# Band attention on one core: where the key projection and the modulation steps run between the scores

## Chip, cores and metric

The kernel runs on one core of one Trainium2 chip. Time is device time in microseconds (us); a run's time is that of the one core. Lower is better.

## The reference

A trunk of two layers on 512 tokens of width 1024: a gated linear recurrence with a feed-forward block, then chunked band attention with a feed-forward block. Every sub-layer has an RMS norm whose scale and shift come from a conditioning vector `c`. The part that matters here is the attention, 16 heads of width 64:

```python
k, v = jnp.split(u_kv @ w_kv, 2, axis=-1)          # one shared K/V
q = u @ w_q
s = jnp.einsum('bqhd,bkhd->bhqk', qc, kb) * scale + bias   # chunk of 64, own + 8 past chunks
s = jnp.where(valid, s, MASK_VALUE)
p = jax.nn.softmax(s, axis=-1)
o = jnp.einsum('bhqk,bkhd->bqhd', p, vb)
mix = o @ w_o
h = h + g1 * mix                                   # g1, sc2, sh2, ... = c_act @ mod_w + mod_b
u = modulate(rms_norm(h, norm_ffn), sh2, sc2)      # input of the feed-forward block
```

All inputs are float32 and the kernel keeps that precision: each matrix product is made of three products of reduced-precision parts.

## The kernel before

Activations lie transposed, channels on the 128 partitions, in 8 tiles `h[j]` of 128x512. A weight block is 8 tiles of 128x128. It is loaded as one 128x1024 row block (`raw`, 512 KB, asked for on SyncE's DMA queue), and `split` makes two parts of it: the high part `wh` on ScalarE (ACT, L147) and the low part `wl = raw - wh` on VectorE (DVE, L153). `mm3` (L239 to L241) then issues three matmuls for each of the 8 tiles: high x high, high x low of the activation, low x high. A projection of 512 tokens is thus 8 steps of 3 matmuls of 512 columns. Each of `raw`, `wh` and `wl` has three buffers, so the part of one weight block waits for the block three before it.

The program is traced in the order in which the Python code runs. A planner then orders each engine's instructions by that order, but moves a later one ahead where, by the planner's own times, the earlier one is not ready yet. `tc.issue_after(ins)` holds the instructions traced under it, where they run on the engine of `ins`, behind `ins`. On the chip each engine runs its list in that order.

**Attention** (L1509 to L1686) is one loop over 64 units: 16 heads times 4 blocks of 128 queries, so 8 units for a pair of heads. In unit k the loop traces

- `scores(hd, i)`: two matmuls of the query part with the high and the low key part (L1572, L1573), then on DVE the bias and row maximum (L1576), on ACT the exponential (L1579), on DVE the reciprocal and the scaling of the rows (L1580, L1581);
- `transposes` of the unit three before (L1590) and their copy to SBUF (L1595 on ACT, L1597 on DVE);
- five units behind the last of a pair, `output(p)`: 16 matmuls with the values (L1604);
- at some units (`MODS_AT`) one step of `side`, described below;
- projection steps from the generator `bfiller`: values, then for each pair p the key projection `("k", p)`, the key copies, the query projection `("bq", p)`, the query copies, and behind pair 7 the first six steps of output blocks 0 to 2 (`("bo", n)`). `CREDIT` and `RATES` say how many steps a unit takes: 3.5 up to unit 16, then 2.0 up to unit 56, then 1.5. A step of three matmuls belongs to one `yield`. `hold` keeps the copies of a pair back until its buffers can be free.

The query copies (L1553 to L1556) make, for head a, `ta` = [high part; low part] and the same for head b in `tb`: ACT writes the high part of `ta`, ACT the high part of `tb`, then DVE the low part of `ta` (L1555) and the low part of `tb` (L1556). All four read the one PSUM tile `pq`. The first score of a pair needs `ta` whole.

Behind the loop comes the **output projection**: for each of 8 output blocks n the rest of its matmuls (blocks 0 to 2 have two steps left, block 3 onwards all eight, with the weights split in `proj`), then on DVE the residual (L405), on ACT the square (L283, for n = 0 L279), on DVE the sum of squares (L286), and the split of the scaled input of the feed-forward block (`us3h` on ACT, L320; its low part on DVE, L321). Then `early_pair` starts the feed-forward block (tiles named `e_f`).

**Modulation steps.** `mod_vectors(("sc2b", "sh2b"))` is a generator, `side`, of 16 steps after a first call that only asks for a row. A step asks for the next 512 KB row of the modulation matrix on SyncE's queue (L378, two buffers) and multiplies the present one on DVE with a sum over the row (L389, tile `mw`), held behind the DVE instruction in `state["mods_after"]`. Before, `MODS_AT` makes 13 calls within the loop (four in each of pairs 0 and 1, one in each of pairs 2 to 6), so 12 steps, and the remaining four are taken in the output projection, behind the residuals of blocks 0 to 3.

Of the kernel before, what the change touches and what calls it, by code (L numbers as in the profile page):

```python
# [12 lines left out]
AF = mybir.ActivationFunctionType  # L13
# [46 lines left out]
HELD, FREE, MOVED = (6, 7), 12, (3, 4)  # L60


V1_AFTER, CREDIT, RATES = 1, 3.0, (3.5, 16, 2.0, 56, 1.5)


KEEP = 5
# [9 lines left out]
def trunk(ctx: ExitStack, tc: tile.TileContext, d, out):  # L76
# [49 lines left out]
    def by_transfer(key):  # L126

        if key[0] == f"f{OUT}" and key[1] == "o":
            return key[2] in MOVED
        return key[0] in [f"f{layer}" for layer in FAST] and key[1] == PLAIN - 1  # L130

    def split(raw, nk, n, nm, tag, key):
        if key in spare:
            wh, wl = spare.pop(key)()
        elif key[:2] == (f"f{OUT}", "o") and key[2] in HELD:
            wh, wl = (wp.tile([P, SHIFT + D], F32R, tag=tag + x, name=f"{nm}_{x}")[:, NEAR:NEAR + nk * n]
                      .rearrange("p (k c) -> p k c", k=nk) for x in "hl")
        else:
            wh = wp.tile([P, nk, n], F32R, tag=tag + "h", name=f"{nm}_h")
            wl = wp.tile([P, nk, n], F32R, tag=tag + "l", name=f"{nm}_l")  # L140
        if by_transfer(key):
            A.activation(wl, raw, AF.Copy, scale=-1.0)
            state["moved"] = G.dma_start(out=wl, in_=raw, accum_op=ALU.add)
        with ExitStack() as pinned:
            if "unit" in state and key[0] in ("k", "bq"):
                pinned.enter_context(tc.issue_after(state["mods_after"].ins))
            A.activation(wh, raw, AF.Copy)  # L147

            state.pop("meanwhile", lambda: None)()
            if key == ("ao", 0):  # L150
                pinned.enter_context(tc.issue_after(state["advanced"].ins))
            if not by_transfer(key):
                low = V.tensor_sub(wl, raw, wh)  # L153
        if not by_transfer(key):
            if key[0] in ("av", "g", "zf", "q", "ao") or key[1] == "o":
                state["mods_after"] = low
        return wh, wl
# [75 lines left out]
    def mm3(ps, w, kt, u, start, stop):  # L233
        wh, wl = w
        uh, ul = u
        with ExitStack() as pinned:
            if "behind" in state:
                pinned.enter_context(tc.issue_after(state["behind"].ins))
            T.matmul(ps, wh[:, kt, :], uh, start=start, stop=False)  # L239
        T.matmul(ps, wh[:, kt, :], ul, start=False, stop=False)  # L240
        T.matmul(ps, wl[:, kt, :], uh, start=False, stop=stop)  # L241

    def proj(key, u, res, ahead=SPLIT_AHEAD):
        w = weight(key, ahead)
        ps = bank("_".join(str(x) for x in key))
        for kt in range(KT):
            mm3(ps, w, kt, u[kt], kt == 0, kt == KT - 1)
            if kt == KT - 1:
                res.append(ps)
            yield  # L250
# [144 lines left out]
    def drain(gen):  # L395
        for _ in gen:
            pass
# [4 lines left out]
        return a  # L402

    def residual(j, ps, g, c=slice(0, S)):
        state["residual"] = V.scalar_tensor_tensor(h[j][:, c], ps[:, c], g[:, j:j + 1], h[j][:, c], op0=ALU.mult,  # L405
                                                   op1=ALU.add)

    def fast_inputs(fp, rb, a, sh, nm):

# [1099 lines left out]
    with tc.tile_pool(name="attn", bufs=1) as ap:  # L1509
# [17 lines left out]
        def qk(p):  # L1527
# [22 lines left out]
            yield p  # L1550
            ta = ap.tile([P, S], F32R, tag="ta", name=f"ta{p}", bufs=2)
            tb = ap.tile([P, S], F32R, tag="tb", name=f"tb{p}", bufs=2)
            A.activation(ta[Q1], pq[Q1], AF.Copy, scale=sc)  # L1553
            A.activation(tb[Q2], pq[Q2], AF.Copy, scale=sc)
            V.scalar_tensor_tensor(ta[Q2], pq[Q1], sc, ta[Q1], op0=ALU.mult, op1=ALU.subtract)  # L1555
            V.scalar_tensor_tensor(tb[Q1], pq[Q2], sc, tb[Q2], op0=ALU.mult, op1=ALU.subtract)  # L1556
            heads[2 * p] = (ta, ka, kla)
            heads[2 * p + 1] = (tb, kb, klb)
# [7 lines left out]
        def scores(hd, i):  # L1566
# [2 lines left out]
            nm = f"{hd}_{i}"  # L1569
            ps = bank("s" + nm)  # L1570
            c = slice(i * P, (i + 1) * P)
            T.matmul(ps[:, 0:n], tq[:, c], kk[:, 0:n], start=True, stop=False)  # L1572
            T.matmul(ps[:, 0:n], tq[:, c], kl[:, 0:n], start=False, stop=True)  # L1573
            s = sm.tile([P, S], F32, tag=("sq", "ut")[i % 2], name="sb" + nm, bufs=2)
            st = ap.tile([P, 4], F32, tag="st", name="st" + nm, bufs=4)
# [76 lines left out]
        part = []  # L1652
        fill = bfiller()
        side = mod_vectors(("sc2b", "sh2b"))
        LAG, LAG2 = 3, 4
        MODS_AT = ((0, 2, 4, 6),) * 2 + ((2,),) * 5 + ((),) * 2
        units = [(hd, i) for hd in range(BH) for i in range(NB)]
        live = {}
        credit = CREDIT
# [5 lines left out]
        for k in range(len(units) + LAG2 + 1):  # L1665
# [17 lines left out]
            while credit >= 1 and (hold is None or k >= 8 * (hold - 1) - 1):  # L1683
                hold = next(fill, None)
                credit -= 1
        drain(fill)  # L1686
        acc = sm.tile([P, S], F32, tag="nacc", name="acc3", bufs=1)
        a_f1 = gain_scale(C_NF + KT, mod["sc2b"], "a_f1")
        shifts[("f1", 0, 0)] = shifts[("f1", 0, 1)] = mod["sh2b"]
        us = []  # L1690
        for n in range(KT):
# [8 lines left out]
            residual(n, ps, mod["g1b"])  # L1700
            square_into(acc, n, "n3")
            us.append(scaled(n, a_f1[:, n:n + 1], "us3"))
            if n < 4:
                state["mods_after"] = state["residual"]
                next(side, None)
            if n == 3:
                drain(side)

                with tc.issue_after(state["scaled"].ins):
                    A.activation(csig[:, 0:1], cols[:, 0:1], AF.Silu)  # L1710
# [236 lines left out]
```

## Time and profile before

| | before |
|---|---|
| median of 3 runs | 1224.31 us (1223.09 to 1225.62) |
| profiled execution, its own time | 1226.39 us |
| its span, first to last instruction | 1224.3 us |
| granted TensorE clock, mean | 0.995 |
| PE / DVE / ACT busy | 1202.3 / 1011.0 / 671.3 us |
| attention loop from the first score to the last output | 677 to 840 us |
| output projection to the first `e_f` matmul | 840 to 881 us |

The profile is one execution of the program. Engines: PE is TensorE's matmuls, PEld its weight loads, DVE VectorE, ACT ScalarE, POOL GpSimd, SPq SyncE's DMA queue. A line number such as L1555 is that of the kernel before. In a timeline row stand the start, the duration, engine, line, operation, output and inputs, shape, and in brackets the idle time of that engine just before and what ended it. Matmuls are pipelined: a 512-column matmul is shown with 0.39 us, and the next one starts earlier than that.

### The profile page before, as it was taken

The page shows a single profiled execution, that of the slowest core. Times are in us where ns is not written, and L with a number is a line of the kernel's source. Part 1 is how long each engine was busy: PE and PEld are TensorE (multiplying, and loading weights), DVE is VectorE, ACT ScalarE, POOL GpSimd, SP SyncE. Part 2 cuts the span into 40 slices and gives each one's busy share as a digit, 9 for nine tenths or more (in the row PEclk, how much of TensorE's full clock was granted, in tenths as well). Part 3 has the DMA queues.
Part 4 walks back from the last instruction along what each step waited for, and adds up shares of the span by engine and source line. Part 5 has one row for each costly group of instructions (what it writes and reads, how often), then busy time and mean ns, then how long its engine had stood idle before and what let it go on. Part 6 is the DMA issues. An engine that isn't in the chain of part 4 may idle for free.

```text
span 1224.3 us, 22314 instructions
## 1 busy us (share of the span) xinstructions
PE 1202.3 (98%) x8758; PEld 1054.2 (86%) x8758; DVE 1011.0 (83%) x1821; ACT 671.3 (55%) x1204; POOL 51.1 (4%) x59
## 2 busy tenths in 40 slices
PE   8999999999999999999999999997999999999997
PEld 6887788888899999988888877775789999998997
DVE  8997778788989999986689778896787888887984
ACT  6455446444656566742238566674455656666553
POOL 0100000000000000000001101010000000001100
PEclk9999999999999999999999999998999999999999
DMA  9642354364423433468766977682634556446842
GB/s 354 251 131 99 114 180 156 108 214 162 131 96 136 138 127 139 143 222 271 239 217 175 276 215 196 195 211 89 194 97 156 189 199 203 168 137 153 228 121 95
DMA packets 71402, 211.94 MB, mean 173 GB/s; under 512 B 7553, under 2 KB 10241, under 8 KB 71297
## 3 DMA queue, kind: packets, MB, share of 16 engines
q1 hardware_dynamic: 63952, 194.27, 46.7%
q0 software_dynamic: 7200, 15.99, 7.9%
q8 instruction: 68, 1.11, 0.4%
q14 instruction: 38, 0.30, 0.1%
q10 hardware_dynamic: 144, 0.26, 0.1%
HBM read 204.99 MB, written 20.97 MB: 185 GB/s over the span
## 4 chain that ended last, share of the span: by engine, by line
PE 82%; DVE 9%; ACT 4%; issue 2%; DMA 2%; SPq 0%; POOLq 0%; ACTq 0%; DVEq 0%
PE f_r L642 9%; PE f_r L641 9%; PE f_r L640 9%; PE f_o L240 4%; PE f_o L241 4%; PE f_o L239 4%; PE f_or L832 2%; PE f_or L831 2%; PE f_or L830 2%; PE o L1162 1%; PE g L239 1%; PE g L241 1%; PE av L262 1%; PE f L241 1%; PE ao L239 1%
## 5 line engine op out<-in xcount | busy, mean ns | idle before, releaser
L642 PE MATMUL f_r<-f_h,f_w_l 128*128 128x256 f32 x1008 | 278.7, 276 | 0.0
L641 PE MATMUL f_r<-f_l,f_w_h 128*128 128x256 f32 x1008 | 278.7, 276 | 0.0
L640 PE MATMUL f_r<-f_h,f_w_h 128*128 128x256 f32 x1008 | 278.7, 276 | 0.0
L641 PEld LDWEIGHTS f_r<-f_l,f_w_h 128*128 128x128 f32 x1008 | 189.5, 188 | 0.1
L640 PEld LDWEIGHTS f_r<-f_h,f_w_h 128*128 128x128 f32 x1008 | 189.3, 188 | 0.1
L642 PEld LDWEIGHTS f_r<-f_h,f_w_l 128*128 128x128 f32 x1008 | 189.3, 188 | 0.0
L389 DVE SCALAR_TENSOR_TENSOR mw<-mw,crow 128x1024 f32<-128x1024 f32 x96 | 115.6, 1219 | 0.4 <-DMA mw<-in_modw 0.4
L590 ACT ACTIVATE f_w_h<-f_x 128x1024 fp32r<-128x1024 f32 x72 | 76.8, 1066 | 50.6 <-PE f_r L641 39.1
L591 DVE TENSOR_TENSOR f_w_l<-f_x,f_w_h 128x1024 fp32r<-128x1024 f32 x72 | 88.2, 1226 | 8.6 <-ACT f_w_h L590 5.2
L591 DVE TENSOR_TENSOR f_w_l<-r_f_c,f_w_h 128x1024 fp32r<-128x1024 f32 x72 | 68.8, 955 | 22.9 <-ACT f_w_h L590 22.9
L590 ACT ACTIVATE f_w_h<-r_f_c 128x1024 fp32r<-128x1024 f32 x72 | 61.1, 849 | 46.6 <-PE f_r L641 46.6
L147 ACT ACTIVATE f_o_h<-r_f_o 128x1024 fp32r<-128x1024 f32 (+2 forms) x39 | 34.3, 891 | 70.5 <-PE f_o L240 48.5
L240 PE MATMUL f_o<-f_p,f_o_h 128*128 128x512 f32 x176 | 68.6, 390 | 0.0
L241 PE MATMUL f_o<-f_p,f_o_l 128*128 128x512 f32 x176 | 68.5, 390 | 0.0
L239 PE MATMUL f_o<-f_p,f_o_h 128*128 128x512 f32 x176 | 68.3, 389 | 0.0
L1579 ACT ACTIVATE sb<-sb,st 128x128 f32<-128x128 f32 (+1 forms) x64 | 35.8, 560 | 37.3 <-DVE st L1578 36.6
L153 DVE TENSOR_TENSOR f_o_l<-r_f_o,f_o_h 128x1024 fp32r<-128x1024 f32 (+2 forms) x35 | 36.1, 1035 | 22.4 <-ACT f_o_h L147 22.1
L1065 DVE TENSOR_TENSOR kq<-kq,t 128x1024 f32<-128x1024 f32 x28 | 34.2, 1222 | 8.1 <-PE l L1132 3.3
L241 PEld LDWEIGHTS f_o<-f_p,f_o_l 128*128 128x128 f32 x176 | 33.0, 188 | 7.4 <-DVE f_o_l L153 0.5
L240 PEld LDWEIGHTS f_o<-f_p,f_o_h 128*128 128x128 f32 x176 | 33.0, 188 | 7.0 <-DVE f_p L542 0.3
L239 PEld LDWEIGHTS f_o<-f_p,f_o_h 128*128 128x128 f32 x176 | 33.0, 188 | 6.8
L241 PE MATMUL f<-f_h,f_l 128*128 128x512 f32 x96 | 36.9, 391 | 0.1
(517 smaller groups left out, 3220.5 us busy)
## 6 DMA issues: line engine op xcount, KB each, us to landing
mw<-in_modw SPq DMA_DIRECT2D x96, 512.0 KB, 4.4
r_f_c<-in_ffn_in SPq DMA_DIRECT2D x72, 512.0 KB, 3.4
ws<-in_ffn_in SPq DMA_DIRECT2D x18, 512.0 KB, 6.4
ws<-in_ffn_in POOLq DMA_DIRECT2D x18, 512.0 KB, 8.3
f_x<-ws SPq DMA_DIRECT2D x36, 256.0 KB, 2.8
mrow<-in_modw SPq DMA_DIRECT2D x16, 512.0 KB, 8.2
r_f<-in_ffn_in SPq DMA_DIRECT2D x16, 512.0 KB, 4.1
r_f_o<-in_ffn_out SPq DMA_DIRECT2D x16, 512.0 KB, 3.5
```

The source lines that it names most:

```text
L147: A.activation(wh, raw, AF.Copy)
L153: low = V.tensor_sub(wl, raw, wh)
L239: T.matmul(ps, wh[:, kt, :], uh, start=start, stop=False)
L240: T.matmul(ps, wh[:, kt, :], ul, start=False, stop=False)
L241: T.matmul(ps, wl[:, kt, :], uh, start=False, stop=stop)
L389: V.scalar_tensor_tensor(mw, mw, 1.0, crow, op0=ALU.mult, op1=ALU.mult, accum_out=raw[:, j:j + 1])
L590: A.activation(wh, raw, AF.Copy)
L591: V.tensor_sub(wl, raw, wh)
L640: T.matmul(ps, wh[:, j, :], uh, start=f, stop=False, skip_group_check=True)
L641: T.matmul(ps, wh[:, j, :], ul, start=False, stop=False, skip_group_check=True)
L642: T.matmul(ps, wl[:, j, :], uh, start=False, stop=stop and j == 3, skip_group_check=True)
L1579: A.activation(s[:, 0:n], s[:, 0:n], AF.Exp, bias=st[:, 1:2], accum_out=st[:, 2:3])
```

## The change

Four edits.

1. In the attention loop, at the last unit of pairs 1 to 5, the generator is drawn until step 4 of the next but one key projection has been traced (`FIRST = 4`, so 5 steps, 15 matmuls), and the first score matmul of pairs 2 to 6 is held behind the last of these. The rate for units 16 to 55 goes from 2.0 to 1.375 steps a unit, so the remaining 3 key steps and 8 query steps of a pair are spread over its 8 units.
2. The query copies are traced in the order: high part of `ta`, low part of `ta`, high part of `tb`, low part of `tb`.
3. The high part of the weights of output block 2 is held behind the high part of `ta` (of pair 7), its low part behind the low part of `ta`.
4. `MODS_AT` has one more step in each of pairs 2 to 5, which makes 17 calls: all 16 steps lie in the loop, and `drain(side)` stands ahead of the output projection; the four steps behind the residuals of blocks 0 to 3 are gone.

```diff
-V1_AFTER, CREDIT, RATES = 1, 3.0, (3.5, 16, 2.0, 56, 1.5)
+V1_AFTER, CREDIT, RATES = 1, 3.0, (3.5, 16, 1.375, 56, 1.5)
@@ split
+            if key == ("bo", 2):
+                pinned.enter_context(tc.issue_after(state["queries"][0].ins))
             A.activation(wh, raw, AF.Copy)
...
+            if key == ("bo", 2):
+                pinned.enter_context(tc.issue_after(state["queries"][1].ins))
             if not by_transfer(key):
                 low = V.tensor_sub(wl, raw, wh)
@@ mm3
-        T.matmul(ps, wl[:, kt, :], uh, start=False, stop=stop)
+        return T.matmul(ps, wl[:, kt, :], uh, start=False, stop=stop)
@@ proj
-            mm3(ps, w, kt, u[kt], kt == 0, kt == KT - 1)
+            state["fill"] = key, kt, mm3(ps, w, kt, u[kt], kt == 0, kt == KT - 1)
@@ qk
-            A.activation(ta[Q1], pq[Q1], AF.Copy, scale=sc)
+            state["queries"] = (
+                A.activation(ta[Q1], pq[Q1], AF.Copy, scale=sc),
+                V.scalar_tensor_tensor(ta[Q2], pq[Q1], sc, ta[Q1], op0=ALU.mult, op1=ALU.subtract))
             A.activation(tb[Q2], pq[Q2], AF.Copy, scale=sc)
-            V.scalar_tensor_tensor(ta[Q2], pq[Q1], sc, ta[Q1], op0=ALU.mult, op1=ALU.subtract)
             V.scalar_tensor_tensor(tb[Q1], pq[Q2], sc, tb[Q2], op0=ALU.mult, op1=ALU.subtract)
@@ scores
-            T.matmul(ps[:, 0:n], tq[:, c], kk[:, 0:n], start=True, stop=False)
+            with ExitStack() as pinned:
+                if state["fill"][0] == ("k", hd // 2 + 1) and not hd % 2 and not i:
+                    pinned.enter_context(tc.issue_after(state["fill"][2].ins))
+                T.matmul(ps[:, 0:n], tq[:, c], kk[:, 0:n], start=True, stop=False)
@@ the loop over units
-        LAG, LAG2 = 3, 4
-        MODS_AT = ((0, 2, 4, 6),) * 2 + ((2,),) * 5 + ((),) * 2
+        LAG, LAG2, FIRST = 3, 4, 4
+        MODS_AT = ((0, 2, 4, 6),) * 2 + ((2, 4),) * 4 + ((2,),) + ((),) * 2
...
+            if at == 7 and 0 < p < KT - 2:
+                while state["fill"][:2] != (("k", p + 2), FIRST):
+                    hold = next(fill, None)
         drain(fill)
+        drain(side)
@@ output projection
-            if n < 4:
-                state["mods_after"] = state["residual"]
-                next(side, None)
             if n == 3:
-                drain(side)
```

`residual` no longer keeps its instruction in `state["residual"]`, which nothing else used.

More of the change, by code (lines that the diff above doesn't have):

```diff
@@ L404, in residual @@
     def residual(j, ps, g, c=slice(0, S)):
-        state["residual"] = V.scalar_tensor_tensor(h[j][:, c], ps[:, c], g[:, j:j + 1], h[j][:, c], op0=ALU.mult,
-                                                   op1=ALU.add)
+        V.scalar_tensor_tensor(h[j][:, c], ps[:, c], g[:, j:j + 1], h[j][:, c], op0=ALU.mult, op1=ALU.add)
     def fast_inputs(fp, rb, a, sh, nm):
```

## Prediction

> **What bounds the kernel now.** I read the head of the page first: which engine is busy, and who ends the chain of waits.
>
> ```profile
> span 1224.3 us, 22314 instructions
> PE 1202.3 (98%) x8758; PEld 1054.2 (86%) x8758; DVE 1011.0 (83%) x1821; ACT 671.3 (55%) x1204; POOL 51.1 (4%) x59
> PE 82%; DVE 9%; ACT 4%; issue 2%; DMA 2%; SPq 0%; POOLq 0%; ACTq 0%; DVEq 0%
> ```
>
> TensorE (PE) sets the time; only 22 us of the span are not PE's by the page, and 9% of the chain is VectorE (DVE). The change touches no arithmetic, so it can gain only what PE waits or runs slow inside attention and the output projection behind it. The view by stretches, cut at the first score of a head pair and around the start of the output projection, says where that is:
>
> ```profile
> core 0: us, PE busy (x) PEld busy (x) DVE busy (x) ACT busy (x) POOL busy (x), PEclk, DMA share, GB/s
> 762.25:781.25 19.00, 18.59 (x101) 14.38 (x101) 15.52 (x53) 12.93 (x30) 1.54 (x2) 1.00 0.77 193
> 800.25:820.30 20.05, 19.18 (x102) 14.67 (x103) 19.14 (x58) 15.90 (x36) 3.16 (x3) 1.00 0.85 225
> 842.87:857.62 14.75, 8.52 (x27) 6.17 (x26) 12.10 (x17) 6.24 (x9) 0.00 (x0) 0.77 0.57 195
> ```
>
> A pair of heads (first row: pair 4) costs 19.0 us and PE idles a little in it. In pair 6 (second row) DVE is at 95%. In the third stretch PE is busy 8.5 of 14.75 us and its granted clock falls to 0.77: that is the big hole. PE's timeline gives both places exactly (columns: start, duration, and in brackets the idle time before it and who ended it):
>
> ```profile
> 725.87 0.33 PE L1572 MATMUL s<-ka,ta 128*128 128x128 f32 x1 [0.25 <-DVE ta L1555]
> 762.25 0.33 PE L1572 MATMUL s<-ka,ta 128*128 128x128 f32 x1 [0.43 <-DVE ta L1555]
> 781.25 0.33 PE L1572 MATMUL s<-ka,ta 128*128 128x128 f32 x1 [0.41 <-DVE ta L1555]
> 800.25 0.33 PE L1572 MATMUL s<-ka,ta 128*128 128x128 f32 x1 [0.41 <-DVE ta L1555]
> 820.30 0.33 PE L1572 MATMUL s<-ka,ta 128*128 128x128 f32 x1 [0.87 <-DVE ta L1555]
> ```
>
> ```profile
> 844.72 0.39 PE L239 MATMUL bo<-oh,bo_h 128*128 128x512 f32 x1
> 845.40 0.39 PE L240 MATMUL bo<-ol,bo_h 128*128 128x512 f32 x1
> 847.92 0.50 PE L239 MATMUL bo<-oh,bo_h 128*128 128x512 f32 x1 [2.12 <-ACT bo_h L147]
> 848.26 0.39 PE L240 MATMUL bo<-ol,bo_h 128*128 128x512 f32 x1
> 852.75 0.80 PE L241 MATMUL bo<-oh,bo_l 128*128 128x512 f32 x1 [4.11 <-DVE bo_l L153]
> 857.62 0.41 PE L240 MATMUL bo<-ol,bo_h 128*128 128x512 f32 x1
> 872.17 0.39 PE L239 MATMUL bo<-oh,bo_h 128*128 128x512 f32 x1
> 881.01 0.39 PE L239 MATMUL e_f<-us3h,f_h 128*128 128x512 f32 x1
> ```
>
> From 872.17 to 881.01 lie 39 matmuls of 512 columns: 0.227 us each, start to start. A shown duration of 0.39 overlaps the next, so 0.16 us is added to each bracket to get PE time lost. First scores of pairs 2, 4, 5, 6, 7 lose 0.41, 0.59, 0.57, 0.57, 1.03: 3.17 us together, all on the scaled query's low part (ta, L1555). In the second fence, 844.72 is the first matmul of output block n = 3 and 881.01 is the first behind block 7: 5 blocks of 24 = 120 matmuls, 27.2 us at 0.227. They take 36.29, so **9.1 us** are lost: two waits (2.29 and 4.26, start to start) and 11 steps of 0.44 instead of 0.227 behind them (2.4). PE works on the high halves of three blocks and then stands until the low half of block 3's weights (bo_l, L153) exists.
>
> **Part 1: all 16 modulation steps inside attention; none in the output projection.** Why bo_l was late is in the timelines of DVE and ScalarE (ACT):
>
> ```profile
> 842.64 2.01 ACT L147 ACTIVATE bo_h<-r_bo 128x1024 fp32r<-128x1024 f32 x2 [1.46 <-PE bo L240]
> 845.08 0.71 ACT L320 ACTIVATE us3h<-h,a_f 128x512 fp32r<-128x512 f32 x1
> 842.87 0.75 DVE L405 SCALAR_TENSOR_TENSOR h<-bo,mod_g1b,h 128x512 f32<-128x512 f32 x1 [0.96 <-PE bo L241]
> 843.54 1.21 DVE L389 SCALAR_TENSOR_TENSOR mw<-mw,crow 128x1024 f32<-128x1024 f32 x1
> 845.35 1.21 DVE L389 SCALAR_TENSOR_TENSOR mw<-mw,crow 128x1024 f32<-128x1024 f32 x1
> 849.08 1.21 DVE L389 SCALAR_TENSOR_TENSOR mw<-mw,crow 128x1024 f32<-128x1024 f32 x1
> 851.48 3.49 DVE L153 TENSOR_TENSOR bo_l<-r_bo,bo_h 128x1024 fp32r<-128x1024 f32 x3
> ```
>
> bo_h of block 3 is finished at about 843.7 (half of the first row), but its low half runs on DVE only at 851.48, behind three modulation products (mw) of 1.21 us and the residuals, squares and splits of blocks 0 to 2. In program order all of these stand ahead of bo_l; the planner takes the earliest ready one, and with the products in the row DVE never ran dry. Without them: residual 0 ends at 843.54; residual 1 can run about 843.6 to 844.3 (PE closes block 1 six matmuls before 844.72); the next item in order, the split of block 0, needs us3h, not ready before 845.79. So DVE is empty at 844.3 and takes bo_l of block 3: 844.3 to 845.5. PE needs it at 844.72 + 2 x 0.227 = 845.18, and two high-half matmuls of block 4 can fill in. bo_l of block 4 has until 850.6; DVE's six other items of 0.75 at most fit before it with nothing to spare. I leave 0.6 us of waits for both: gain 9.1 - 0.6 = **8.5 us**. Ends: 9.1 (nothing left), and 1.6 if DVE keeps its order without filling the gap (second rival). I take a value near the upper end, as DVE's own rows leave it empty there. The fourth product (behind block 3) hid beside PE; nothing for it.
>
> The clock decides 2.4 of the 9.1. A shorter gap further on bears on this:
>
> ```profile
> 886.40 1.05 PE L291 MATMUL n_ss<-mean,acc 128*128 128x1 f32 x8 [1.15 <-DVE acc L286]
> 888.70 0.63 PE L241 MATMUL e_f<-us3h,f_l 128*128 128x512 f32 x1
> 891.26 0.63 PE L241 MATMUL e_f<-us3h,f_l 128*128 128x512 f32 x1
> ```
>
> Between 888.70 and 891.26 six steps take 0.427 each: a slow stretch after a gap of 1.3 us and eight one-column matmuls. So a left-over wait could still bring slow steps; at 0.6 us I expect none, and 2.4 more lost is the lower end (gain 6.1). The Trainium skill, "TensorE: Matmul & The Clock Gate", section on HAM oscillation, says that only PE-idle gaps over about 3.4 us bring the half clock back. By that rule a wait of 0.6 us costs only itself (8.5 stands); by the row at 886.40 it could cost up to 2.4 more; the gap of 4.3 us at 852.75 agrees with the rule, the one at 886.40 is shorter than it allows.
>
> The four products move into pairs 2 to 5, one more each: 1.21 us and a result read of 0.08 on DVE, 15.52 + 1.3 = 16.8 of about 18.4 us per pair (91%). Their weight rows (4 x 512 KB) are asked for earlier on SyncE's queue, with a row buffer that the pair before has freed. On PE's path this costs nothing as long as DVE stays ahead; pair 6 ran at 95% and lost PE time only at its end. I charge 0.1 us in each of five pairs, 0.5 in all, between 0 and the 0.57 that a pair loses today. Nearest is 0: in the stretch that gets tighter I put the first query-weight matmul that needs a low half at about 4.9 us behind the pair's first score (three units with their transposes 1.8, three key steps 2.2, the fourth score 0.5, two matmuls 0.5). Its low half in pair 5:
>
> ```profile
> 784.77 1.22 DVE L153 TENSOR_TENSOR bq_l<-r_bq,bq_h 128x1024 fp32r<-128x1024 f32 x1
> ```
>
> It ends at 785.99, 4.74 behind the score at 781.25. That was needed 8 us behind before; now it is just in time. Whatever is late there costs tenths.
>
> **Part 2: 15 key matmuls ahead of a pair's first score (pairs 2 to 6), the rest one step to a unit.** PE's work is the same, only its order changes. Today the planner put 11 matmuls ahead of pairs 4 to 6 and 15 or 16 ahead of pairs 2 and 3. Four more are 0.91 us, over the 0.57 to 0.59 lost in pairs 4 to 6: covered. Pair 2 has its 16 already; there part 3 must do it.
>
> **Part 3: the query's low part between the two copies.**
>
> ```profile
> 798.29 0.58 ACT L1553 ACTIVATE ta<-bq 64x512 fp32r<-64x512 f32 x1
> 798.88 0.59 ACT L1554 ACTIVATE tb<-bq 64x512 fp32r<-64x512 f32 x1
> 799.51 0.68 DVE L1555 SCALAR_TENSOR_TENSOR ta<-bq,ta 64x512 fp32r<-64x512 f32 x1 [0.40 <-ACT tb L1554]
> 816.52 1.05 ACT L147 ACTIVATE bo_h<-r_bo 128x1024 fp32r<-128x1024 f32 x1
> 818.23 1.22 DVE L153 TENSOR_TENSOR bo_l<-r_bo,bo_h 128x1024 fp32r<-128x1024 f32 x1
> 819.56 0.69 DVE L1555 SCALAR_TENSOR_TENSOR ta<-bq,ta 64x512 fp32r<-64x512 f32 x1
> ```
>
> ta's low part does not need tb, yet the third row waits for it (both read one PSUM tile). With the low part issued between them it can start 0.3 to 0.6 us sooner; head b's query is ready no later. So pair 2's 0.41 is covered as well. Pair 7 has no key matmuls. There bo_l of block 2 (fifth row) sits ahead of ta; pinned behind it, it frees 1.2 us: ta's low part would run 818.8 to 819.5, against 819.56 to 820.25. With bo_h out of the way on ACT somewhat sooner still. Of the 1.03 I take 0.85. bo_l of block 2 then runs later in pair 7, where its matmuls come behind two others; no cost.
>
> Sum for parts 2 and 3: 0.41 + 0.59 + 0.57 + 0.57 + 0.85 = 3.0. All together 8.5 + 3.0 - 0.5 = **11.0 us**. The sum is made in the execution with the span of 1224.3 us, which took 1226.39 with what lies around it; the median of three runs is 1224.31. Taken off that median: **1213.3**.
>
> **Rivals.**
> 1. *DVE keeps the old order at the tail* (residuals, squares and splits of blocks 0 to 2, then bo_l). Only the products drop out, and the splits still wait for ACT: bo_l would start between 847.9 (851.48 - 3 x 1.21) and 849.9. PE gains 1.6 to 3.6 there, and perhaps 1.5 of slow steps. With 2.5 from the pairs: about 1218. For it: the planner's times are not the chip's. Against it: DVE has nothing else at 844.3.
> 2. *DVE becomes the bound in pairs 2 to 5.* If its idle time stays at 19.00 - 15.52 = 3.5 us, a pair takes 16.8 + 3.5 = 20.3 us, 1.3 longer than now: 4 x 1.3 = 5.2 lost instead of 2 gained; with the tail's 8.5 and pair 7's 0.85, about 1220. For it: DVE and ACT take their items in the planned order and wait for each other (0.40 ahead of 799.51). Against it: the 5.5 us of projections between a pair's last score and the next pair's first now let DVE run clear.
> 3. *Slower: the row loads hold up weight loads.* SyncE's queue is in order, and a row load stands until DVE has used the row two before it:
>
> ```profile
> SPq L378 <- DVE mw L389: 58.2, 12, 24.9
> ```
>
> 12 such waits, up to 24.9 us. If in pairs 2 to 5 a key or query weight is asked for behind one and lands late, PE waits openly. It decides from 11 / 4 = 2.75 us a pair; with 5 us a pair it is 1224.3 - 11.0 + 20 = 1233. Against it: today's long wait falls in a stretch with nothing else to ask for, and high halves are made nearly a pair early.
> 4. *Part 2 does nothing* because ACT's copies are late by as much as the score: 1.7 us less gain, 1215.0, inside the first case's range.
>
> **How the numbers follow.** The forecast case (both holes closed, 1210 to 1216.5, with the fourth rival in it) 0.64; rival 1 (1216.5 to 1219.5) 0.18; rival 2 (1219 to 1223) 0.09; rival 3 0.04; better than 1210 0.05, since DVE may also be less late ahead of the gap at 886.40 (1.3 us and 1.3 of slow steps). The range 1209.0 to 1219.5 holds the first two and most of the last. 0.2% is 2.4 us, about what a measurement of this kernel tells from none (three runs spread over 2.5). Faster by more: 0.64 + 0.18 + 0.05 + 0.03 of rival 2 = 0.90; within: 0.06; slower: 0.04.
>
> **What would show it.** The profile after should have no bracket over 0.2 us at the first scores of pairs 2 to 7; no product (L389) between the last attention output and block 3; bo_l of block 3 on DVE within 2 us of its bo_h; granted clock 1.00 through the output projection, and about 27.5 us from block 3's first matmul to the first behind block 7. Wrong would be: DVE still full from residual 0 to bo_l of block 3, pairs 3 to 5 of 19 us or more, or PE waiting for bq_l or k_l inside a pair.

## The result and the profile after

The change takes 0.73% off: median 1214.97 us (1213.83 to 1216.16, six runs) against 1223.84 us for the kernel before (1222.39 to 1225.62, six runs). The ratio is 0.9927, 95% interval 0.9915 to 0.994. The forecast was 1213.3 us, with a range of 1209.0 to 1219.5. The time is near the forecast, but the profile shows that the output projection gave somewhat more than forecast and attention, forecast 2.5 us shorter, became 0.9 us longer, so the parts are read one by one. Line numbers of the kernel after are 2 to 7 higher than before: L239 to L241 are L243 to L245, L389 is L393, L1555 is L1558.

The head of the page after, with the shares of the chain of waits:

```profile
span 1213.6 us, 22300 instructions
PE 1199.2 (99%) x8758; PEld 1052.1 (87%) x8758; DVE 1008.5 (83%) x1821; ACT 670.4 (55%) x1204; POOL 51.0 (4%) x59
PE 85%; DVE 7%; ACT 2%; issue 2%; DMA 2%; SPq 0%; POOL 0%; POOLq 0%; ACTq 0%; DVEq 0%
```

PE is idle in 14 us of the span, where before it was in 22. The view by stretches, cut as before, at the first scores of pairs 4, 5, 6 and 7, and from block 3 of the output projection to the first `e_f`:

```profile
core 0: us, PE busy (x) PEld busy (x) DVE busy (x) ACT busy (x) POOL busy (x), PEclk, DMA share, GB/s
763.44:782.37 18.93, 18.45 (x102) 14.41 (x101) 16.06 (x54) 12.47 (x30) 1.25 (x2) 1.00 0.82 202
782.37:801.30 18.93, 18.45 (x101) 14.42 (x101) 16.06 (x54) 12.47 (x30) 2.17 (x2) 1.00 0.71 208
801.30:820.04 18.74, 17.13 (x93) 12.62 (x92) 17.26 (x57) 15.31 (x36) 1.06 (x1) 1.00 0.76 227
846.06:873.26 27.20, 27.20 (x122) 22.41 (x121) 23.43 (x41) 15.05 (x22) 2.09 (x2) 1.00 0.68 196
```

The last row is the output projection: 27.20 us and PE busy in all of them at full clock, where before took 36.29. The big hole is closed to the last tenth. DVE and ACT at its place:

```profile
844.22 1.43 DVE L409 SCALAR_TENSOR_TENSOR h<-bo,mod_g1b,h 128x512 f32<-128x512 f32 x2 [0.94 <-PE bo L245]
845.57 1.22 DVE L157 TENSOR_TENSOR bo_l<-r_bo,bo_h 128x1024 fp32r<-128x1024 f32 x1
846.70 0.75 DVE L409 SCALAR_TENSOR_TENSOR h<-bo,mod_g1b,h 128x512 f32<-128x512 f32 x1
843.99 2.01 ACT L149 ACTIVATE bo_h<-r_bo 128x1024 fp32r<-128x1024 f32 x2 [1.44 <-PE bo L244]
```

Two residuals, then `bo_l` of block 3, then the third residual: the order that the prediction worked out.

The first three rows of the stretches are the surprise. A pair still takes 18.93 us, with half a microsecond of PE idle in it. PE's waits moved from the pair's first score to its query projection:

```profile
730.97 0.51 PE L245 MATMUL bq<-uqh,bq_l 128*128 128x512 f32 x1 [0.22 <-DVE st L1585]
750.11 0.50 PE L245 MATMUL bq<-uqh,bq_l 128*128 128x512 f32 x1 [0.28 <-DVE bq_l L157]
769.05 0.50 PE L245 MATMUL bq<-uqh,bq_l 128*128 128x512 f32 x1 [0.48 <-DVE bq_l L157]
787.98 0.50 PE L245 MATMUL bq<-uqh,bq_l 128*128 128x512 f32 x1 [0.48 <-DVE bq_l L157]
806.91 0.50 PE L245 MATMUL bq<-uqh,bq_l 128*128 128x512 f32 x1 [0.48 <-DVE bq_l L157]
818.18 0.50 PE L244 MATMUL bo<-ol,bo_h 128*128 128x512 f32 x1 [0.94 <-DVE ol L1629]
820.04 0.33 PE L1579 MATMUL s<-ka,ta 128*128 128x128 f32 x1 [0.19 <-DVE ta L1558]
```

The waits at the first scores are gone except for pair 7 (last row). In their place PE waits in each of pairs 2 to 6 at its first matmul with the low half of the query weights, and once at the end of pair 6 for the low part of an attention output. With 0.16 us for each bracket, as in the prediction, that is 4.2 us, more than the 3.17 us that were there before. Of it 2.7 us stand at `bq_l` and 1.45 us ahead of pair 7.

### The profile page after: what moved, and what is told of

Its sections match the earlier page's. It is cut to its first block, busy times and chain, and to the rows that moved or that the text cites. A ratio compares the mean times of both kernels' runs of the same rounds, so it can differ in the third digit from the quotient of the medians.

```text
span 1213.6 us, 22300 instructions
## 1 busy us (share of the span) xinstructions
PE 1199.2 (99%) x8758; PEld 1052.1 (87%) x8758; DVE 1008.5 (83%) x1821; ACT 670.4 (55%) x1204; POOL 51.0 (4%) x59
## 3 DMA queue, kind: packets, MB, share of 16 engines
q8 instruction: 68, 1.11, 0.4%
## 4 chain that ended last, share of the span: by engine, by line
PE 85%; DVE 7%; ACT 2%; issue 2%; DMA 2%; SPq 0%; POOL 0%; POOLq 0%; ACTq 0%; DVEq 0%
PE f_r L644 9%; PE f_r L645 9%; PE f_r L643 9%; PE f_o L244 4%; PE f_o L243 4%; PE f_o L245 4%; PE f_or L835 2%; PE f_or L834 2%; PE f_or L833 2%; PE bo L1611 1%; PE av L266 1%; PE f L245 1%; PE f L243 1%; PE bo L243 1%; PE f L244 1%
## 5 line engine op out<-in xcount | busy, mean ns | idle before, releaser
L393 DVE SCALAR_TENSOR_TENSOR mw<-mw,crow 128x1024 f32<-128x1024 f32 x96 | 115.7, 1219 | 2.0 <-DMA mw<-in_modw 2.0
L245 PE MATMUL f_o<-f_p,f_o_l 128*128 128x512 f32 x176 | 68.5, 390 | 0.0
L243 PE MATMUL f_o<-f_p,f_o_h 128*128 128x512 f32 x176 | 68.3, 389 | 0.0
L245 PEld LDWEIGHTS f_o<-f_p,f_o_l 128*128 128x128 f32 x176 | 33.0, 188 | 7.4 <-DVE f_o_l L157 0.5
L243 PEld LDWEIGHTS f_o<-f_p,f_o_h 128*128 128x128 f32 x176 | 33.0, 188 | 6.8
L245 PE MATMUL f<-f_h,f_l 128*128 128x512 f32 x96 | 36.9, 391 | 0.3 <-DMA f_l<-r_f 0.3
```

Source lines behind the costliest of these rows:

```text
L245: return T.matmul(ps, wl[:, kt, :], uh, start=False, stop=stop)
L393: V.scalar_tensor_tensor(mw, mw, 1.0, crow, op0=ALU.mult, op1=ALU.mult, accum_out=raw[:, j:j + 1])
```

## The experiments

For each run two lengths of the profile are given: **attention**, from the first score of pair 0 to the start of the last group of value matmuls, and the **tail**, from there to the first `e_f` matmul. Each ratio is to runs of the kernel before that were made together with the run's own.

| run | median us | ratio to before, 95% | attention | tail |
|---|---|---|---|---|
| before (lengths of its first profile) | 1223.84 | 1 | 161.08 | 42.85 |
| after | 1214.97 | 0.9927 (0.9915 to 0.994) | 162.01 | 33.73 |
| e1 steps only | 1213.08 | 0.992 (0.9907 to 0.9932) | 160.39 | 33.72 |
| e2 order only | 1221.03 | 0.9982 (0.9973 to 0.9991) | 159.04 | 42.97 |
| e3 old queries | 1214.97 | 0.9935 (0.9923 to 0.9948) | 162.33 | 33.72 |
| e4 steps late | 1212.43 | 0.9913 (0.9899 to 0.9926) | 160.55 | 33.77 |
| e5 before again | 1222.83 | one run | 161.01 | 42.79 |
| e6 steps behind block 3 | 1211.73 | 0.9911 (0.9896 to 0.9926) | 159.38 | 33.77 |
| e7 one step left | 1219.24 | 0.9973 (0.9961 to 0.9984) | 159.35 | 39.68 |
| e8 steps later | 1212.64 | 0.9917 (0.9902 to 0.9932) | 159.01 | 34.46 |
| e9 late, old queries | 1213.55 | 0.9918 (0.9904 to 0.9931) | 160.54 | 33.76 |
| e10 second at 3 | 1215.43 | 0.9935 (0.9922 to 0.9947) | 162.08 | 33.78 |
| e11 second at 6 | 1213.35 | 0.9918 (0.9904 to 0.9931) | 160.21 | 33.74 |
| e12 second at 0 | 1218.24 | 0.9957 (0.9944 to 0.9969) | 164.78 | 33.72 |

An interval reaches some 1.5 us to either side, so differences below about 2 us between two of these medians are not told apart; the lengths are read from one execution each and are finer.

**e1: part 1 alone.** The kernel before, with the new `MODS_AT`, `drain(side)` ahead of the output projection, and no steps in it.

```diff
-        MODS_AT = ((0, 2, 4, 6),) * 2 + ((2,),) * 5 + ((),) * 2
+        MODS_AT = ((0, 2, 4, 6),) * 2 + ((2, 4),) * 4 + ((2,),) + ((),) * 2
+        drain(side)
-            if n < 4:
-                state["mods_after"] = state["residual"]
-                next(side, None)
             if n == 3:
-                drain(side)
```

> The kernel before with the 16 modulation steps inside attention (MODS_AT and drain as after), nothing else. Theory A (the products alone closed the hole in the output projection): block 3 to the first e_f matmul takes 27.2 to 28 us instead of 36.3, the gap ahead of the row sums goes as well, and the whole is 1211 to 1214, as fast as the full change or a little faster, because the rest gained nothing. Rival B (the new score order carries part of it): 1216 or more, with 1 to 3 us still lost in the projection or at the first scores.

Measured: 0.992, so part 1 alone is at least as fast as the whole change. The tail is 33.72 us, the same as after. And with the old order of matmuls the four extra products cost nothing in attention: 160.39 us, 0.7 less than before. In this order the first matmul with `bq_l` comes 7.7 to 8.4 us behind a pair's first score, and `bq_l` ends at 4.53, so there is room. Three first scores still wait (0.42, 0.61 and 0.31 us with the 0.16, pairs 2, 3 and 7).

**e2: parts 2 and 3 alone.** The kernel after, with twelve steps in the loop and four behind residuals 0 to 3, as before.

```diff
-        MODS_AT = ((0, 2, 4, 6),) * 2 + ((2, 4),) * 4 + ((2,),) + ((),) * 2
+        MODS_AT = ((0, 2, 4, 6),) * 2 + ((2,),) * 5 + ((),) * 2
-        drain(side)
+            if n < 4:
+                state["mods_after"] = state["residual"]
+                next(side, None)
             if n == 3:
+                drain(side)
```

(In e2, e6 and e7 `residual` keeps its instruction in `state["residual"]` again.)

> The changed kernel with the modulation steps as before (12 in the loop, four in the output projection). Theory A (the low half of the next query weights comes just too late for PE because the score order and the query order moved its need forward and its making back): still 0.3 to 0.7 us of PE wait for bq_l in pairs 3 to 6, attention no shorter than before, the hole in the projection as before, whole 1222 to 1226. Rival C (the four extra products on VectorE are what delays it): waits for bq_l under 0.2 us, attention 2 to 3 us shorter than before, whole 1219 to 1222.

Measured: attention 159.04 us, 2.04 less than before. A pair without the extra product:

```profile
780.89:799.36 18.47, 18.47 (x102) 14.37 (x100) 15.10 (x52) 12.54 (x29) 1.04 (x1) 1.00 0.64 183
```

PE is busy in the whole of it; the forecast implied 19.00 - 0.57 = 18.43. So the new order does what it was costed for, and adding the four products to it costs 162.01 - 159.04 = 2.97 us. The waits that come with them are 2.36 us at `bq_l` in pairs 3 to 6 and 0.81 us more ahead of pair 7 (pair 2's 0.38 us is there in e2 too), 3.17 us together. Neither part is at fault alone; they collide.

**e3: part 3 undone**, the query copies back in their old order, the rest as after.

```diff
-            state["queries"] = (
-                A.activation(ta[Q1], pq[Q1], AF.Copy, scale=sc),
-                V.scalar_tensor_tensor(ta[Q2], pq[Q1], sc, ta[Q1], op0=ALU.mult, op1=ALU.subtract))
+            high = A.activation(ta[Q1], pq[Q1], AF.Copy, scale=sc)
             A.activation(tb[Q2], pq[Q2], AF.Copy, scale=sc)
+            state["queries"] = (high, V.scalar_tensor_tensor(ta[Q2], pq[Q1], sc, ta[Q1], op0=ALU.mult,
+                                                             op1=ALU.subtract))
```

> The changed kernel with the query copies in the old order (both high parts on ScalarE, then both low parts on VectorE). Theory A: VectorE no longer idles 0.66 us between the two low parts, the first softmax of a pair and bq_l come 0.3 to 0.5 us earlier behind the first score, PE's wait for bq_l falls from 0.64 to 0.2 or less, but the first score may wait up to 0.3 us again for ta; whole 0 to 2 us faster than the changed kernel (1213 to 1215). Rival D (the query order is what covers the first scores, as forecast): first scores wait 0.3 us or more in each of pairs 2 to 7 and the whole is 1 to 3 us slower than the changed kernel.

Measured: 1214.97 us, attention 0.32 us longer than after: not told apart in time. Pair 2's first score waits 0.42 us again (with the 0.16), as it does in e1 and e9 and in no kernel with the new order of copies. So part 3 removes that wait. The waits at `bq_l` fall to 0.22 to 0.37 us a pair, though, and the one ahead of pair 7 for the attention output rises to 1.40; what part 3 is worth is e9's question.

**e4: the four extra steps late**, in and behind pair 7.

```diff
-        MODS_AT = ((0, 2, 4, 6),) * 2 + ((2, 4),) * 4 + ((2,),) + ((),) * 2
+        MODS_AT = ((0, 2, 4, 6),) * 2 + ((2,),) * 5 + ((0, 4),) + ((0, 2),)
```

> The changed kernel with the four extra steps not in pairs 2 to 5 but two in pair 7 and two behind it, where VectorE has 5 us and more of idle time. Rival C (the extra products delay bq_l): waits for bq_l gone, 1211 to 1213. Theory A (order, not load): waits for bq_l within 0.2 us of those of the changed kernel, whole within 1 us of it, unless the products reach into the output projection again and bring back part of its hole.

Measured: 0.9913; pairs 3 to 5 take 18.46 to 18.51 us without a wait, as in e2, and the tail stays at 33.77. Taking the second product out of pairs 2 to 5 brings their time back. Pair 2 has a wait of its own here (1.27 us at the same matmul), and PE waits 0.70 us ahead of pair 7 for the low part of an attention output.

**e5: the kernel before, profiled again.** No edit.

> The kernel before, unchanged, profiled a second time. In the profile of before the stretch from the first fast-layer matmul (e_f) to n_b is 15.75 us, in the four kernels with the change or a part of it 12.78 to 12.87, and DVE waited 4.41 us there for a row load (r_f). Theory A: that load was late in this one execution and the change has no part in it: the stretch is again 12.8 us, the span 1221 to 1222 and attention 161 us, with the hole of 9.1 us unchanged. Rival: the hole in the output projection makes that load late: 15 to 16 us again, and a part of the change's gain lies there.

The load was late in the first execution only. DVE's wait for it, in the first profile of before, in the second, and after:

```profile
873.43 0.29 DVE L213 TENSOR_SCALAR wsh_f<-r_f,mod_sh2b 128x128 f32<-128x128 f32 x1 [4.41 <-DMA r_f<-in_ffn_in]
```

```profile
871.14 0.29 DVE L213 TENSOR_SCALAR wsh_f<-r_f,mod_sh2b 128x128 f32<-128x128 f32 x1 [2.72 <-DMA r_f<-in_ffn_in]
```

```profile
863.01 0.29 DVE L217 TENSOR_SCALAR wsh_f<-r_f,mod_sh2b 128x128 f32<-128x128 f32 x1 [2.32 <-DMA r_f<-in_ffn_in]
```

From the first `e_f` to `n_b` the second profile has 12.79 us, and every other run has 12.79 to 12.89; the first had 15.75. The gap and the slow steps at 886.40 to 891.26, quoted in the prediction, were that execution's own: in the second profile the granted clock is 1.00 there. The span is 1220.8 us, 7.2 more than after, and the budget closes: the tail is 9.06 us longer, attention 1.00 shorter, and attention starts 0.91 us sooner (that start scatters by 1.2 us between all these profiles, ahead of anything changed), in sum 7.15 us.

**e6: place or load?** The new order, and the four steps behind blocks 3 to 6 of the output projection, not 0 to 3.

```diff
-            if n < 4:
+            if 3 <= n < 7:
                 state["mods_after"] = state["residual"]
                 next(side, None)
+            if n == 6:
+                drain(side)
             if n == 3:
-                drain(side)
```

This diff is against e2.

> The new order of matmuls and queries, twelve steps inside attention, and the four others behind blocks 3 to 6 of the output projection and not behind 0 to 2. Theory A (the hole is a matter of place: the products stood ahead of block 3's low half on an engine that never ran dry): the hole closes as in the changed kernel, 27.2 to 28.5 us from block 3 to the first e_f, pairs of 18.5 us as in the run with the order alone, 1210.5 to 1213 in all. Rival (a matter of load: DVE cannot take four more products in that stretch at all): DVE is busy 23.4 of 27.2 us there without them, with 4.9 us more it overflows; blocks 5 to 7 then wait for their low halves or the first e_f for its input, 29 to 32 us, 1215 to 1218 in all.

Measured: 1211.73 us, the lowest median of all. From block 3 to the first `e_f`:

```profile
842.53:869.69 27.16, 27.16 (x122) 22.35 (x120) 24.88 (x39) 14.85 (x22) 2.09 (x2) 1.00 0.80 251
```

All four products stand in this stretch, DVE is busy for 24.88 of its 27.16 us (after, without them, 23.43 of 27.20), and PE never waits. The hole was a matter of place.

**e7: one step left** behind residual 0.

```diff
-        MODS_AT = ((0, 2, 4, 6),) * 2 + ((2, 4),) * 4 + ((2,),) + ((),) * 2
+        MODS_AT = ((0, 2, 4, 6),) * 2 + ((2,),) * 5 + ((0, 4),) + ((0,),)
-        drain(side)
+            if n < 1:
+                state["mods_after"] = state["residual"]
+                next(side, None)
+                drain(side)
```

> The new order, fifteen steps inside attention (the last two in its last pair), and one behind block 0 of the output projection where before had four. Theory A (threshold: one product of 1.21 us at residual 0 is enough for DVE never to run dry, so that block 3's low half stays behind the splits of blocks 0 to 2): a hole of 3 us or more, half the clock possibly with it, 30 to 35 us from block 3 to the first e_f, 1215 to 1220 in all. Rival (dose: each product delays that half by its own 1.21 us and no more): 0 to 1.2 us lost, 27.2 to 28.5 us, 1212.5 to 1214.

Measured: 1219.24 us. One product of 1.22 us costs 5.9 us of tail (39.68 against 33.77 in e4, which has this one step in the loop). DVE first, then PE:

```profile
841.37 0.75 DVE L409 SCALAR_TENSOR_TENSOR h<-bo,mod_g1b,h 128x512 f32<-128x512 f32 x1 [0.94 <-PE bo L245]
842.04 1.22 DVE L393 SCALAR_TENSOR_TENSOR mw<-mw,crow 128x1024 f32<-128x1024 f32 x1
843.18 0.75 DVE L409 SCALAR_TENSOR_TENSOR h<-bo,mod_g1b,h 128x512 f32<-128x512 f32 x1
847.11 0.74 DVE L325 SCALAR_TENSOR_TENSOR us3l<-h,a_f,us3h 128x512 fp32r<-128x512 f32 x1
847.77 3.48 DVE L157 TENSOR_TENSOR bo_l<-r_bo,bo_h 128x1024 fp32r<-128x1024 f32 x3
```

```profile
847.55 0.50 PE L243 MATMUL bo<-oh,bo_h 128*128 128x512 f32 x1 [3.27 <-ACT bo_h L149]
847.88 0.40 PE L244 MATMUL bo<-ol,bo_h 128*128 128x512 f32 x1
849.03 0.80 PE L245 MATMUL bo<-oh,bo_l 128*128 128x512 f32 x1 [0.75 <-DVE bo_l L157]
849.63 0.63 PE L243 MATMUL bo<-oh,bo_h 128*128 128x512 f32 x1
851.34 0.63 PE L244 MATMUL bo<-ol,bo_h 128*128 128x512 f32 x1
```

Behind residual 0 comes the product, then residuals, squares and splits without a break, and only then the low halves: DVE does not run dry once, so `bo_l` of block 3 stays where program order put it. It starts 4.56 us behind block 3's first matmul (843.21), after 0.49 us ahead of it. This is no dose: one product costs 5.9 us, and all four, in e2, 9.2 (42.97 against 33.73). PE waits 3.43 and 0.91 us (with the 0.16), and from 849.03 to 851.76 six steps take 0.43 to 0.60 us in place of 0.227; the last section takes up the clock behind them.

**e8: sixteen steps at other units.**

```diff
-        MODS_AT = ((0, 2, 4, 6),) * 2 + ((2, 4),) * 4 + ((2,),) + ((),) * 2
+        MODS_AT = ((0, 2, 4, 6), (0, 2, 4)) + ((2,),) * 4 + ((), (0, 2, 4, 6), (0, 2))
```

> The changed kernel with its sixteen steps at other units: four and three in pairs 0 and 1 (the last unit of pair 1 freed), one each in pairs 2 to 5, none in pair 6, four in pair 7, two behind. Theory A (a product shortly ahead of a pair's start sets DVE's chain back, and in pair 7 there is room): pair 2 has its wait of 1.27 us for a softmax statistic no more, pair 7 starts with less than 0.3 us of wait for the low half of an attention output, pairs 18.5 us, attention 159 to 160 us, 1211.0 to 1212.0 in all. Rival (pair 7 and the last units are full too, 17.26 of 18.74 us of DVE there in the changed kernel): pair 7 lengthens by 1 us or more or the hole in the output projection comes back, 1212.5 to 1216.

Measured: 1212.64 us, 0.6 above the range of the first theory, at the rival's lower edge. (The 17.26 of 18.74 us in the rival are pair 6's row above, not pair 7's.) In the trace the first theory holds for pair 7 (no wait ahead of it, no hole behind) and half for pair 2: 0.61 us at the same matmul and not 1.27. In time it is not told apart from e4, whose two lengths sum to 194.3 us against 193.5 here. The tail is 0.7 us longer, because the last value group takes 3.05 us and not 2.30: the second head's matmuls start at 836.48, 0.76 us behind the first's, where the two heads start together in every other run's last group; ACT's copy of a `pt` ends at 836.43.

**e9: the steps of e4 and the old order of the query copies** (the diffs of e4 and e3 together).

> Part 3 where no extra product disturbs it: the kernel with the steps late (two each in pairs 0 and 1's four units, one in pairs 2 to 6, the last four in pair 7 and behind), with the old order of query copies and low parts and the new pins. Theory A (15 key matmuls ahead of the first score do all the covering, the copy order is worth nothing in pairs 2 to 6): within 0.5 us of the run with the steps late (1212.4), first scores of pairs 3 to 6 without a wait. Rival (the low part of the scaled query is late again without its early place): 0.2 to 0.4 us at each of five first scores, 1213.5 to 1214.5.

Measured: 1213.55 us, in the rival's range by the median, but with a ratio (0.9918) that is not told apart from e4's (0.9913); attention takes 160.54 us against e4's 160.55. No gain from part 3 is seen here in sum. First scores wait in pair 2 (0.41 us with the 0.16) and pair 7 (0.31), in none of pairs 3 to 6: these two are what the order of copies covers, as the prediction said. But what e4 gains by it comes back in pair 2 at the query weights, where e4 waits 1.27 us and e9 0.33.

**e10, e11, e12: the second product of a pair elsewhere**, at unit 3, 6 or 0 in place of 4. The edit of e10 (the others have `(2, 6)` and `(0, 2)`):

```diff
-        MODS_AT = ((0, 2, 4, 6),) * 2 + ((2, 4),) * 4 + ((2,),) + ((),) * 2
+        MODS_AT = ((0, 2, 4, 6),) * 2 + ((2, 3),) * 4 + ((2,),) + ((),) * 2
```

> The changed kernel with the second step of pairs 2 to 5 at unit 3 and not at unit 4, so that its product of 1.21 us runs some 2.3 us sooner, 8 us and not 6 us ahead of the next pair's first score. Theory A (place: the product sets back DVE's chain of low parts and statistics at the end of the pair, and DVE has 2.5 us of slack to make it up if it comes sooner): pairs 3 to 5 of 18.5 us, no wait for bq_l, 1212.0 to 1213.5 in all. Rival (dose: two products a pair are too many wherever they stand): pairs of 18.9 us, 1214.5 to 1216.

> The changed kernel with the second step of pairs 2 to 5 at unit 6, nearer to the next pair's first score. Theory A (place): the low parts of the queries and with them bq_l come later still, pairs of 19.1 us or more with a wait at the first score or at bq_l of over 0.64 us, 1215.5 to 1219 in all. Rival (dose): pairs of 18.9 us as at unit 4, 1214.5 to 1215.5. Third: the product falls into a stretch in which DVE waits 1.46 us for a softmax exponential anyway, and the pair is 18.5 us, 1212 to 1213.

> The changed kernel with the second step of pairs 2 to 5 at the pair's first unit. Theory A (place): the product runs ahead of bq_l, which PE needs 5 us behind the first score, so PE waits 0.6 to 1.3 us there in each of four pairs, pairs of 19.0 to 19.7 us, 1215 to 1218 in all. Rival (dose): pairs of 18.9 us, 1214.5 to 1215.5.

My theory of place falls for units 3 and 6. At unit 3 (1215.43 us, in the rival's range) pairs 4 and 5 take 18.95 and 18.93 us, as at unit 4. At unit 6 (1213.35 us, below the ranges of theory A and the rival) it is not worse but mixed: pairs 3 and 5 take 18.93 and 18.91, pair 4 takes 18.51 with the same products in it. At unit 0 (1218.24 us) place does decide: pairs 3 to 5 take 19.87 us each. The product (787.45 in pair 5) runs ahead of `bq_l`, which ends 6.67 us behind the first score and not 5.00 as in e6. Of the 1.4 us a pair, 0.6 shows as a wait for a scaled softmax row, not for `bq_l` as expected. The rest lies inside the group of value matmuls, without a bracket: with one query matmul among them they take 3.52 us in e12's pair 5 (791.37 to 794.89), and 2.30 + 0.23 in e6 (786.26 to 788.56, and one matmul). In e6 the two heads' value matmuls start in twos; in e12 they start apart from 792.28 on. What holds them apart was not looked into.

Pair 4 and pair 5 of e11, the same kernel with the same products, show what goes with the 0.5 us: the order that the planner gave a few neighbours. ACT ahead of pair 4's first score (763.15), then ahead of pair 5's (781.66):

```profile
759.00 0.72 ACT L1586 ACTIVATE sb<-sb,st 128x512 f32<-128x512 f32 x1 [0.68 <-DVE st L1585]
759.73 1.06 ACT L149 ACTIVATE k_h<-r_k 128x1024 fp32r<-128x1024 f32 x1
760.70 0.57 ACT L1557 ACTIVATE ta<-bq 64x512 fp32r<-64x512 f32 x1
```

```profile
778.22 1.06 ACT L149 ACTIVATE k_h<-r_k 128x1024 fp32r<-128x1024 f32 x1 [1.36 <-PE bq L244]
779.19 0.71 ACT L1586 ACTIVATE sb<-sb,st 128x512 f32<-128x512 f32 x1
779.89 0.57 ACT L1557 ACTIVATE ta<-bq 64x512 fp32r<-64x512 f32 x1
```

In the first, the pair's last exponential goes ahead of the high half of the next key weights (`k_h`). In the second it goes behind `k_h`, which has to wait for PE to free its buffer. On DVE, too, the product (777.49) stands ahead of the small statistic that the exponential needs (778.63), in pair 4 behind it. So the exponential starts 2.47 us and not 4.15 us ahead of the first score, and everything that hangs on it comes late: the scaling of the row, the low part of `ta`, `tb`, the first row maximum of the new pair, and behind that `bq_l`. In the kernel after it is `k_h` above all (ACT, then DVE, around pair 5's first score at 782.37):

```profile
778.94 1.06 ACT L149 ACTIVATE k_h<-r_k 128x1024 fp32r<-128x1024 f32 x1 [0.43 <-PE bq L244]
779.90 0.71 ACT L1586 ACTIVATE sb<-sb,st 128x512 f32<-128x512 f32 x1
```

```profile
776.35 1.22 DVE L393 SCALAR_TENSOR_TENSOR mw<-mw,crow 128x1024 f32<-128x1024 f32 x1
777.62 0.68 DVE L1583 CUSTOM_DVE_ANT_0 sb<-s,wb 128x512 f32<-128x512 f32 x1
778.62 0.13 DVE L1585 TENSOR_SCALAR st<-st 128x1 f32<-128x1 f32 x1
780.74 0.16 DVE L1587 RECIPROCAL st<-st 128x1 f32<-128x1 f32 x1 [1.46 <-ACT sb L1586]
782.80 0.69 DVE L1560 SCALAR_TENSOR_TENSOR tb<-bq,tb 64x512 fp32r<-64x512 f32 x1 [0.66 <-ACT tb L1559]
786.71 1.22 DVE L157 TENSOR_TENSOR bq_l<-r_bq,bq_h 128x1024 fp32r<-128x1024 f32 x1
```

and in e6, with no second product (its pair starts at 780.35, one line number higher):

```profile
776.47 0.72 ACT L1587 ACTIVATE sb<-sb,st 128x512 f32<-128x512 f32 x1 [0.87 <-DVE st L1586]
777.66 1.05 ACT L149 ACTIVATE k_h<-r_k 128x1024 fp32r<-128x1024 f32 x1
```

After, the second product stands just ahead of the last row maximum (777.62). The statistic is ready at 778.75, 3.6 us ahead of the score, and e6 starts the exponential 3.88 ahead: DVE has nearly made up for the product. But `k_h` holds ACT until 779.9, so the exponential starts 2.47 ahead, and DVE idles 1.46 us for it. Over all kernels with the new order and copies and no product at unit 0 (after, e2, e4, e6, e7, e8, e10, e11), in pairs 3 to 5: 16 pairs have the exponential ahead of `k_h`, `bq_l` ends 5.00 to 5.01 us behind the first score and PE does not wait; 8 have it behind, `bq_l` ends at 5.22 to 5.60 and PE waits 0.28 to 0.52. Pair 2 has it behind in all eight and waits in all eight (0.22 to 1.11). That agreement is read from the traces, and it does not hold with the old order of copies: in e3's pair 4 the exponential also goes behind `k_h`, and `bq_l` ends at 4.53. A run that changes nothing but these two instructions' order was not made, so why the pair loses is shown by e2, e4 and e6 (the second product), and through which step only argued.

## Why the prediction was right or wrong, point by point

- **The hole in the output projection (8.5 us): right**, in size and in mechanism, and the 0.6 us kept back was not needed. It measures 9.06 to 9.09. e1 shows that the four products alone do it, e6 that their place and not their load made the hole, e7 that one of them is enough to bring back two thirds.
- **Parts 2 and 3 (3.0 us): the waits went where stated, a third came back elsewhere.** Alone they gain 2.04 us (e2): the first-score waits vanish, and new ones of 0.38 us (pair 2, query weights) and 0.64 us (ahead of pair 7, attention output) appear: 3.0 - 1.0 = 2.0. Those two places were not looked at as next in line.
- **The four products in pairs 2 to 5 (0.5 us): the step that failed.** They cost 2.97 us (after against e2), six times the term. The prediction found the place: first matmul with `bq_l`, needed 4.9 us behind the first score, `bq_l` ready at 4.74 before, "just in time". In the new order nothing is left of that margin even without the four products: in e2's pair 5 `bq_l` ends 5.00 us behind the first score (780.89), and its matmul starts at 5.05. The prediction then charged 0.1 us a pair; it is 0.44 to 0.64 us in each of pairs 3 to 6, and 0.81 us ahead of pair 7, a place that the charge did not include. The wrong link was "costs nothing as long as DVE stays ahead": DVE's share of busy time (16.06 of 18.93 us) says nothing on a chain that passes from DVE to ACT and back twice. With the old order (e1) they do cost nothing, because `bq_l` is needed about 3 us later there.
- **The gap at 886.40, counted as nothing: right** for the median, since it belonged to one execution (e5).
- **Sum.** 9.1 + 2.0 - 3.0 = 8.1 against 11.0 forecast; the medians moved by 8.87, with an interval of 7.3 to 10.4. The time came near the forecast because the largest term was right. The other terms together were forecast to gain 2.5 us, and attention lost 0.9 (161.08 to 162.01); the whole change is not shown to be faster than its part 1 alone (e1).
- **Rivals.** DVE keeping its old order at the tail (the first in the list, called the second in part 1): wrong for this change, true of e7. DVE the bound in pairs 2 to 5: right in direction and wrong in kind, 0.46 us a pair over e2 where 1.9 was reckoned (20.3 against 18.43), through one late chain and not through a full engine. Row loads holding up weights: no; SyncE's waits of this kind fell in sum and in the longest (whole execution, before and after; the prediction's line was of a part of it):

```profile
SPq L378 <- DVE mw L389: 164.5, 71, 24.9
SPq L382 <- DVE mw L393: 125.5, 63, 6.7
```

- Part 2 without effect: no, the waits at the scores of pairs 4 to 6 are gone.
- **What the prediction said the profile would show**: all of it at the tail, and at the first scores too (the longest bracket is pair 7's 0.19 us); of its signs of being wrong, PE waiting for `bq_l` inside a pair came true.

## What to carry over

When work is taken out of one stretch and put into another, price it at the receiving chain's tightest hand-over, and multiply by how often that comes, not by the engine's mean slack. A product of 1.2 us can cost nothing (e1), 0.5 us (pairs 4 and 5 after) or 5.9 us (e7) depending on what the planner orders around it: put it where its engine has just handed off and nobody waits next, here behind blocks 3 to 6 (0.9911; against after, the profile has 3.6 us less span, though the two intervals overlap). And profile the kernel before twice before a gap in it becomes a term of the sum.

## What the runs showed of the hardware

Slow steps do not follow from one gap's length alone. Before, PE stood 2.29 us ahead of 847.92 and its next step took 0.34 us. In e2 it stood 2.30 us at the same matmul (845.88) and the next step took 0.59.

The granted clock in the traces shows more. In the first profile of before it falls to 0.50 at 850.81, comes back at 857.64, falls again at 888.36 and comes back at 891.77; in e2 it is 0.50 from 845.70 to 855.93, in e7 from 848.60 to 852.01. Within each trace these times lie whole multiples of 3.41 us apart (2, 9 and 1; 3; 1). Cut into stretches of 3.41 us at these times, before:

```profile
843.98:847.39 3.41, 1.81 (x8) 1.15 (x7) 3.41 (x7) 3.41 (x6) 0.00 (x0) 1.00 0.42 153
847.40:850.81 3.41, 0.73 (x2) 0.30 (x2) 3.41 (x6) 1.71 (x3) 0.00 (x0) 1.00 0.44 155
850.82:854.22 3.40, 1.47 (x4) 1.18 (x5) 3.40 (x5) 0.00 (x0) 0.00 (x0) 0.50 0.60 198
```

then e2, then e7:

```profile
842.29:845.70 3.41, 1.45 (x7) 0.87 (x5) 3.41 (x7) 3.41 (x6) 0.00 (x0) 1.00 0.47 160
845.71:849.11 3.40, 1.22 (x2) 0.50 (x2) 3.40 (x7) 1.36 (x3) 0.00 (x0) 0.50 0.45 148
```

```profile
845.19:848.60 3.41, 0.73 (x2) 0.30 (x2) 3.41 (x6) 2.31 (x4) 0.00 (x0) 1.00 0.17 66
```

The first figure behind the length is PE's busy time, the third from the end the granted clock. The gap of before lies across two stretches, with PE busy 1.81 and 0.73 us, and the clock falls only behind the second, inside the next gap. The gap of e2 begins in a stretch with 1.45 us and runs across its end, and there the clock falls. In e7 the step behind the gap of 3.43 us took 0.33 us, at full clock; the clock falls 1 us later, at the end of a stretch with 0.73 us. So where a gap lies against these stretches mattered as well as its length. How busy PE must be in one to keep the clock stays open: it held behind 1.81 us and fell behind 0.73, 1.45 and, at 888.36, 2.26 (eight one-column matmuls among them). No run was made to vary this alone.

The Trainium skill, "TensorE: Matmul & The Clock Gate", section on HAM oscillation, puts the limit at idle gaps over about 3.4 us. Before's gap of 4.26 us is longer than that, but the clock fell when it had lasted 2.2 us; e2's gap of 2.30 us, with the clock at 0.50 when PE resumed, is shorter, and here the measurement decides: in a kernel like this a gap of 2.3 us may already cost more than itself.
